# Rotary difference and sum of the softmax heads formed on VectorE instead of GpSimd

## The chip, the cores and the metric

The kernel runs on one core of one Trainium2 chip. A core has five engines that work side by side, each through its own queue of instructions in a fixed order: TensorE (PE in the profile; its weight loads are PEld), VectorE (DVE), ScalarE (ACT), GpSimd (POOL) and SyncE (SP, which here only issues DMAs). The engines wait for each other through semaphores. The metric is the device time of one execution in microseconds (us), lower is better.

## The reference

A trunk of two layers over 512 positions of width 1024, in float32. Each layer has two groups of attention heads side by side on one input projection: eight stick-breaking heads (called s here) and four differential heads (called d), each of which has two softmax maps. Only the d heads get rotary position embedding. An MLP with squared ReLU follows.

```python
def rope(x, pos):
    ...
    x1, x2 = xf[..., : d // 2], xf[..., d // 2:]
    rot = jnp.concatenate([-x2, x1], axis=-1)
    return (xf * cos + rot * sin).astype(x.dtype)

for l in range(DEPTH):
    h = rmsnorm(x, attn_norm[l])
    proj = jnp.einsum('bsd,de->bse', h, w_in[l])
    sb_q, sb_k, sb_v, df_q, df_k, df_v = jnp.split(proj, splits, axis=-1)
    sb_out = stick_breaking_attention(sb_q, sb_k, sb_v)
    dq, dk = rope(df_q, pos), rope(df_k, pos)
    df_heads = differential_attention(dq, dk, dvv, lam)
    ...
    x = x + jnp.einsum('bse,ed->bsd', mixed, w_o[l])
    h = rmsnorm(x, mlp_norm[l])
    u = jnp.square(jax.nn.relu(jnp.einsum('bsd,df->bsf', h, w_ff1[l])))
    x = x + jnp.einsum('bsf,fd->bsd', u, w_ff2[l])
return rmsnorm(x, final_norm)
```

For a pair of halves (x1, x2) rotation gives x1 cos - x2 sin and x2 cos + x1 sin.

## The kernel before

Activations lie transposed, features on the 128 partitions and the 512 positions along the row, so that every projection block is a 128x512 tile. To keep float32 accuracy each operand of a matmul is split in two: a high part of reduced precision, made by ScalarE as a copy (`hi`), and the rest (`lo`), made by VectorE as a subtraction. A product is then three matmuls (`three`, lines 281 to 283). Weights are streamed from memory through SP's queue into buffers named `raw`, split into `whi` (line 116, ScalarE) and `wlo` (line 117, VectorE), and used some 5 us later.

In each layer a list (`ORDER`) interleaves the projection blocks: four d heads (d0 to d3), each followed by its values (w0 to w3), then the s heads. The generator `dense` emits these blocks; between its steps the attention work `attn` of heads that are ready is emitted in small pieces (scores, softmax, transposes, product with the values). A clock of estimated PE time decides where: `defer(delay, fn)` puts work off until that clock has advanced by `delay`, and `ready` says from when a head's scores may be emitted. What is written so is a program text. The order in which each engine runs its instructions is then set by the framework's planner when the program is built: it takes, of the instructions whose inputs and buffers are there by its own estimate, the one that was emitted first.

The step around the change is `evict_d`. For a d head, the projection was arranged so that one block (named q in the tile names) holds the first halves of both maps' queries and keys, and a second block (named k) holds their second halves. For each block VectorE multiplies the result, still in PSUM, with the cosine (`u`, line 445) and with the sine (`v`, line 446). The tables `cos_t` and `sin_t` also hold the normalisation of the input. When the second block has been multiplied, `rest` is deferred by `DLY_R` (3.5 us). It forms `u1 - v` (line 453) and `v1 + u` (line 454), in place in the first block's tiles; splits both into `hl` (line 224 for the high part on ScalarE, line 225 for the rest on VectorE); and moves the pieces by twelve DMAs on SP's queue (line 420) into the tiles `st` (query; and key, high part) and `kl` (key, rest). In the kernel before, lines 453 and 454 run on GpSimd.

The tiles u and v come from a ring of five buffers (tag "t", `TB = 5`) that the products, the values' `tv` tiles and other row tiles share. A new product waits until a buffer is freed, that is, until `rest` of an earlier head has read it.

What stands near it: the scores (lines 477 and 478) of a head on PE wait for `st` and `kl`; the softmax has a masking memset, a maximum (lines 521 to 526), an exponential on ScalarE (534), a reciprocal and small steps (540, 541) and a weighted sum of the two maps (544), which is transposed on PE (567). The norm of a finished d head sends a power of -1/2 through GpSimd (`rc`, line 259), whose result is cast by VectorE (`chi`, line 260, and `clo`, line 261) and spread by GpSimd into two diagonal tiles (264, 266). In the head d3 this norm, of an earlier head, meets the change's step.

Of the kernel before, what the change touches and what calls it, by code (L numbers as in the profile page):

```python
# [151 lines left out]
def trunk(ctx, tc, xT, w, w2, gains, gfin, lamv, cos, sin, out):  # L152
    nc = tc.nc
# [69 lines left out]
    def split(hi, lo, src):  # L223
        nc.scalar.activation(hi, src, AF.Copy)  # L224
        nc.vector.tensor_tensor(out=lo, in0=src, in1=hi.bitcast(F32), op=ALU.subtract)  # L225
# [91 lines left out]
    for l in range(L):  # L317
        with ExitStack() as actx:
# [18 lines left out]
            def tt(name):  # L337
                return a2.tile([P, S], F32, tag="t", name=name, bufs=TB)
# [4 lines left out]
            def parts(name):  # L343
                return a2.tile([P, 2, 2, S], F32R, tag="hl", name=name)
# [62 lines left out]
            def defer(delay, fn):  # L407
                later.append((clock[0] + delay, fn))
                later.sort(key=lambda e: e[0])

            def stack_tiles(kind, b, which):
                nm = f"{l}{kind}{b}{which}"
                out = [a2.tile([P, 2, S], F32R, tag="st" + which, name="st" + nm)]
                if which == "k":
                    out.append(a2.tile([P, 2, S], F32R, tag="kl", name="kl" + nm))
                stacks[(kind, b, which)] = out
                return out

            def move(dst, src):
                nc.sync.dma_start(dst.bitcast(F32), src.bitcast(F32))  # L420
# [21 lines left out]
            def evict_d(pt, kind, b, which):  # L442
                nm = f"{l}{kind}{b}{which}"
                u, v = tt("u" + nm), tt("v" + nm)
                nc.vector.tensor_mul(u, pt, cos_t)
                nc.vector.tensor_mul(v, pt, sin_t)
                if which == "q":
                    heads[("x", b)] = (u, v)
                    return
                u1, v1 = heads.pop(("x", b))  # L450

                def rest():
                    nc.gpsimd.tensor_sub(u1, u1, v)
                    nc.gpsimd.tensor_add(v1, v1, u)
                    q, = stack_tiles(kind, b, "q")
                    k = stack_tiles(kind, b, "k")
                    hl = parts("hl" + nm)
                    for j, o in enumerate((u1, v1)):
                        split(hl[:, 0, j, :], hl[:, 1, j, :], o)
                        to = slice(64 * j, 64 * j + 64)  # L460
                        for m in range(2):
                            rq = slice(32 * m, 32 * m + 32)
                            rk = slice(64 + 32 * m, 64 + 32 * m + 32)
                            move(q[to, m, :], hl[rq, :, j, :])
                            for half in range(2):
                                move(k[half][to, m, :], hl[rk, half, j, :].unsqueeze(1).to_broadcast([32, 2, S]))
                    ready[(kind, b)] = clock[0] + DLY_D

                defer(DLY_R, rest)
# [299 lines left out]
        with ExitStack() as fctx:  # L769
# [152 lines left out]
            for g in range(GROUPS):  # L922
# [26 lines left out]
                for f, form in enumerate(FORMS):  # L949
# [6 lines left out]
                    for n, (c, i, r) in enumerate(work):  # L956
                        if c not in held:
                            held[c] = W.next("f")
                        u = held[c]
# [154 lines left out]
```

## Time and profile before

| | |
|---|---|
| median of 3 runs | 1173.97 us (1173.69 to 1174.61) |
| the profiled execution | 1170.51 us, of which 1168.7 us are the span of the trace |
| granted clock of PE | 0.997 of full speed |
| lines 453 and 454 | 16 instructions, 128x512 each, on GpSimd, from 33.6 to 86.2 us (layer 0) and from 611.6 to 664.3 us (layer 1) |
| DMA | 170.11 MB moved, 146 GB/s on average |

The profile lists one execution. "Busy" is time in which an engine ran an instruction; matmuls overlap each other, so that PE may be recorded as busy a little beyond what it does. A row of the timeline gives the start, the duration, the engine, the line and operation, the tile written and those read, the shape, and in brackets how long the engine had been idle before and what ended the wait. A row of waits gives who waited, for whom, the sum in us, how often and the longest. SPq is the queue that SP issues DMAs from. The tile names carry layer, kind, head and block: `u0d3q` is u of layer 0, head d3, first block; the rows with `1` are layer 1.

### The profile page before, as it was taken

Reading aid. Unit: us, or ns where it says so; the run is one execution under the profiler, and the core shown is the slowest. Engines: PE = TensorE matmul, PEld = TensorE weight load, DVE = VectorE, ACT = ScalarE, POOL = GpSimd, SP = SyncE. Lnnn points to the kernel's source line nnn. Section 1 sums busy time; section 2 is a strip of 40 time slices with the busy share of each in tenths; the row PEclk is TensorE's granted clock in tenths of the full one; section 3 lists DMA queues with packets and bytes.
Section 4 is the critical chain, followed back from the end, with each engine's and each line's share of the span. In section 5 each row is a group of like instructions: output and inputs, shape, how many; then the busy total and the mean of one; then the engine's idle time right before and its main releaser. Section 6 shows DMA issues by size and latency. Waiting matters only on the chain.

```text
span 1168.7 us, 15328 instructions
## 1 busy us (share of the span) xinstructions
PE 1147.7 (98%) x5454; PEld 952.0 (81%) x5454; DVE 813.0 (70%) x1302; ACT 652.4 (56%) x1153; POOL 213.7 (18%) x282
## 2 busy tenths in 40 slices
PE   9999999999999999999899999999999999999996
PEld 6887888888888888888688878888888888888884
DVE  7888788765545756647789877877655466476568
ACT  6455666556756446455445556655666563554554
POOL 1222443130100101002012215331201010010021
PEclk9999999999999999999999999999999999999999
DMA  7555433255844936837525553432658368276185
GB/s 246 163 151 171 123 113 109 72 190 152 212 136 105 224 128 126 224 95 157 110 72 166 168 153 109 140 96 73 225 122 229 120 124 226 93 168 192 36 173 132
DMA packets 56860, 170.11 MB, mean 146 GB/s; under 512 B 7120, under 2 KB 8144, under 8 KB 56784
## 3 DMA queue, kind: packets, MB, share of 16 engines
q1 hardware_dynamic: 46416, 131.88, 34.6%
q0 software_dynamic: 10224, 37.23, 18.5%
q8 instruction: 43, 0.70, 0.2%
q14 instruction: 33, 0.27, 0.1%
q10 hardware_dynamic: 144, 0.02, 0.0%
HBM read 138.17 MB, written 2.10 MB: 120 GB/s over the span
## 4 chain that ended last, share of the span: by engine, by line
PE 86%; DVE 5%; DMA 2%; issue 2%; ACT 1%; POOL 0%; SPq 0%; POOLq 0%; DVEq 0%; ACTq 0%
PE f L282 10%; PE f L283 10%; PE f L281 10%; PE x L282 4%; PE x L281 4%; PE x L283 4%; PE wo L281 3%; PE wo L282 3%; PE wo L283 3%; DMA q<-in_w 2%; DVE wlo L117 1%; PE T0s L567 1%; PE T1s L567 1%; PE O0s L596 0%; PE O1s L596 0%
## 5 line engine op out<-in xcount | busy, mean ns | idle before, releaser
L117 DVE TENSOR_TENSOR wlo<-raw,whi 128x1024 fp32r<-128x1024 f32 (+1 forms) x130 | 154.6, 1193 | 98.0 <-ACT whi L116 97.4
L117 DVE TENSOR_TENSOR wlo<-q,whi 128x512 fp32r<-128x512 f32 x224 | 146.0, 687 | 106.2 <-ACT whi L116 105.7
L281 PE MATMUL f<-h_hi,whi 128*128 128x512 f32 x512 | 199.6, 390 | 0.0
L283 PE MATMUL f<-h_hi,wlo 128*128 128x512 f32 x512 | 199.3, 389 | 0.0
L282 PE MATMUL f<-h_lo,whi 128*128 128x512 f32 x512 | 199.2, 389 | 0.0
L116 ACT ACTIVATE whi<-q 128x512 fp32r<-128x512 f32 x224 | 129.6, 624 | 120.3 <-PE f L282 38.1
L116 ACT ACTIVATE whi<-raw 128x1024 fp32r<-128x1024 f32 (+1 forms) x130 | 131.5, 1018 | 106.7 <-PE f L282 55.4
L794 POOL DMA_DIRECT2D q<-in_w x64 | 56.0, 878 | 558.1 <-DVE wlo L117 471.9
L281 PEld LDWEIGHTS f<-h_hi,whi 128*128 128x128 f32 x512 | 96.1, 188 | 19.9
L282 PEld LDWEIGHTS f<-h_lo,whi 128*128 128x128 f32 x512 | 96.1, 188 | 19.9
L283 PEld LDWEIGHTS f<-h_hi,wlo 128*128 128x128 f32 x512 | 96.1, 188 | 19.9
L225 DVE TENSOR_TENSOR Al<-F,Ah 128x256 fp32r<-128x256 f32 (+2 forms) x96 | 74.8, 779 | 44.1 <-ACT Ah L224 44.0
L281 PE MATMUL x<-whi,Ah 128*128 128x512 f32 x256 | 100.0, 391 | 0.0
L282 PE MATMUL x<-wlo,Ah 128*128 128x512 f32 x256 | 99.8, 390 | 0.1
L283 PE MATMUL x<-whi,Al 128*128 128x512 f32 x256 | 99.7, 389 | 0.0
L224 ACT ACTIVATE Ah<-F 128x256 fp32r<-128x256 f32 (+2 forms) x96 | 67.6, 704 | 45.7 <-DVE F L830 43.7
L282 PEld LDWEIGHTS x<-wlo,Ah 128*128 128x128 f32 x256 | 48.1, 188 | 10.4 <-DVE wlo L117 0.5
L281 PEld LDWEIGHTS x<-whi,Ah 128*128 128x128 f32 x256 | 48.1, 188 | 10.0
L283 PEld LDWEIGHTS x<-whi,Al 128*128 128x128 f32 x256 | 48.1, 188 | 9.9
L821 ACT ACTIVATE F<-f 128x512 f32<-128x512 f32 x64 | 37.6, 587 | 10.9 <-DVE Al L225 5.4
L822 ACT ACTIVATE F<-F 128x512 f32<-128x512 f32 x64 | 40.3, 630 | 1.5
L228 ACT ACTIVATE h_hi<-x,g_all 128x512 fp32r<-128x512 f32 x32 | 22.6, 718 | 26.1 <-DVE x L704 13.8
(1057 smaller groups left out, 2574.1 us busy)
## 6 DMA issues: line engine op xcount, KB each, us to landing
raw<-in_w SPq DMA_DIRECT2D x126, 512.0 KB, 3.5
q<-in_w SPq DMA_DIRECT2D x64, 512.0 KB, 5.5
q<-in_w POOLq DMA_DIRECT2D x64, 512.0 KB, 6.0
x<-in_xT SPq DMA_DIRECT2D x8, 256.0 KB, 4.3
raw<-in_w SPq DMA_DIRECT2D x8, 128.0 KB, 4.2
yx<-y POOLq DMA_DIRECT2D x2, 512.0 KB, 7.8
y<-y POOLq DMA_DIRECT2D x2, 512.0 KB, 7.7
y<-yx POOLq DMA_DIRECT2D x2, 512.0 KB, 6.0
```

What stands on the lines that cost most here:

```text
L116: h = nc.scalar.activation(hi[:, a:b], raw[:, a:b], AF.Copy)
L117: self.last = h, nc.vector.tensor_tensor(out=lo[:, a:b], in0=raw[:, a:b], in1=hi[:, a:b].bitcast(F32), op=ALU.subtract)
L224: nc.scalar.activation(hi, src, AF.Copy)
L225: nc.vector.tensor_tensor(out=lo, in0=src, in1=hi.bitcast(F32), op=ALU.subtract)
L228: a = nc.scalar.activation(h_hi[:, c, :], x[:, c, :], AF.Copy, scale=g)
L281: nc.tensor.matmul(pt, ah, bh, start=first, stop=False)
L282: nc.tensor.matmul(pt, ah, bl, start=False, stop=False)
L283: nc.tensor.matmul(pt, al, bh, start=False, stop=last)
L567: nc.tensor.transpose(pt[:, off : off + P], u["w"][qi][:, kb * P : (kb + 1) * P], ident)
L794: nc.gpsimd.dma_start(t, quad(g, q, c), accum_op=ALU.add)
L821: nc.scalar.activation(t, pt, AF.Relu)
L822: nc.scalar.activation(t, t, AF.Square)
```

## The change

The two operations of `rest` are issued on VectorE. Nothing else in the text is altered; what comes before and after them is emitted at the same places.

```diff
@@ -450,8 +450,8 @@
                 u1, v1 = heads.pop(("x", b))
 
                 def rest():
-                    nc.gpsimd.tensor_sub(u1, u1, v)
-                    nc.gpsimd.tensor_add(v1, v1, u)
+                    nc.vector.tensor_sub(u1, u1, v)
+                    nc.vector.tensor_add(v1, v1, u)
                     q, = stack_tiles(kind, b, "q")
                     k = stack_tiles(kind, b, "k")
                     hl = parts("hl" + nm)
```

## The prediction

> **What bounds the kernel now.** I read the page's head first, then busy time in stretches of 10 us around the two places where the changed lines run, then what TensorE waited for there, and then the queues of each engine in order of time.
>
> ```profile
> span 1168.7 us, 15328 instructions
> PE 1147.7 (98%) x5454; PEld 952.0 (81%) x5454; DVE 813.0 (70%) x1302; ACT 652.4 (56%) x1153; POOL 213.7 (18%) x282
> ...
> 40.00:50.00 10.00, 9.39 (x48) 7.60 (x47) 9.09 (x17) 4.60 (x13) 3.26 (x2) 1.00 0.73 190
> 50.00:60.00 10.00, 9.62 (x50) 7.81 (x48) 9.26 (x25) 6.06 (x16) 1.29 (x1) 1.00 0.76 236
> 60.00:70.00 10.00, 10.00 (x50) 8.49 (x51) 9.97 (x25) 5.76 (x16) 2.20 (x1) 1.00 0.52 139
> ...
> 90.00:100.00 10.00, 8.65 (x46) 6.83 (x45) 8.55 (x18) 5.07 (x9) 0.00 (x0) 1.00 0.77 222
> ```
>
> TensorE (PE) is busy 98% of the span. The rows of stretches give, after the length, PE, weight load, VectorE (DVE), ScalarE (ACT) and GpSimd (POOL). Where the softmax heads are prepared, DVE is nearly full (9.97 of 10 from 60 to 70) while POOL has room. So nothing that POOL or DVE does counts by itself; it counts where PE stands still. That is rare, and it is listed:
>
> ```profile
> PE S0d L477 <- issue: 1.4, 1, 1.4
> PE p0d2q L283 <- DVE wlo L117: 0.6, 1, 0.6
> PE T0d L567 <- DVE p0d L544: 0.4, 1, 0.4
> ...
> PE S1d L477 <- DMA kl1d3k<-hl1d3k: 1.4, 1, 1.4
> PE vT1w L386 <- DVE tv1w L381: 0.2, 1, 0.2
> PE S1d L478 <- DMA kl1d0k<-hl1d0k: 0.2, 1, 0.2
> ```
>
> The first three are from 30 to 100 us (layer 0), the others from 600 to 680 us (layer 1). Together 4.2 us, and that is almost all that this change can win. The two of 1.4 us are the scores of the last softmax head, d3. A recorded wait understates what is lost, because matmuls overlap:
>
> ```profile
> 94.65 0.40 PE L282 MATMUL p0s0q<-h_lo,whi 128*128 128x512 f32 x1
> 94.89 0.40 PE L283 MATMUL p0s0q<-h_hi,wlo 128*128 128x512 f32 x1
> 96.63 0.36 PE L477 MATMUL S0d<-st0d3k,st0d3q 128*128 128x256 f32 x1 [1.35 <-issue]
> ```
>
> Starts are 0.24 apart in the stream, and this one comes 1.74 after the last: 1.5 us are lost, 0.15 more than the wait says. With 0.15 for each of six waits the whole is about 5.1 us, which is the bound of the gain.
>
> **The change part by part.** Sixteen instructions (a difference, line 453, and a sum, line 454, for four heads in two layers) leave POOL and go to DVE. No DMA is added, and no other work.
>
> *Their own cost.* What they take now and what their like takes on DVE:
>
> ```profile
> 40.99 2.27 POOL L453 TENSOR_TENSOR u0d1q<-u0d1q,v0d1k 128x512 f32<-128x512 f32 x1
> 57.84 1.29 POOL L454 TENSOR_TENSOR v0d2q<-v0d2q,u0d2k 128x512 f32<-128x512 f32 x1 [14.58 <-DVE sm0d L540]
> 82.65 1.30 POOL L454 TENSOR_TENSOR v0d3q<-v0d3q,u0d3k 128x512 f32<-128x512 f32 x1 [18.11 <-ACT whi L116]
> 83.90 1.03 POOL L259 TENSOR_TENSOR rc<-ms,mhalf 128x4 f32<-128x4 f32 x1
> 84.90 1.30 POOL L453 TENSOR_TENSOR u0d3q<-u0d3q,v0d3k 128x512 f32<-128x512 f32 x1
> ...
> 38.93 0.68 DVE L445 TENSOR_TENSOR u0d1k<-p0d1k,cos_t 128x512 f32<-128x512 f32 x1
> 39.52 0.68 DVE L446 TENSOR_TENSOR v0d1k<-p0d1k,sin_t 128x512 f32<-128x512 f32 x1
> 40.12 1.99 DVE L117 TENSOR_TENSOR wlo<-raw,whi 128x1024 fp32r<-128x1024 f32 x1
> 42.04 1.77 DVE L225 TENSOR_TENSOR hl0d1k<-v0d1q,hl0d1k 128x512 fp32r<-128x512 f32 x1
> 43.96 0.69 DVE L225 TENSOR_TENSOR hl0d1k<-u0d1q,hl0d1k 128x512 fp32r<-128x512 f32 x1
> 45.17 1.21 DVE L117 TENSOR_TENSOR wlo<-raw,whi 128x1024 fp32r<-128x1024 f32 x1
> 57.99 1.17 DVE L541 SCALAR_TENSOR_TENSOR sm0d<-top,nlam,sm0d 128x1 f32<-128x1 f32 x1
> 60.65 0.22 DVE L541 SCALAR_TENSOR_TENSOR sm0d<-top,nlam,sm0d 128x1 f32<-128x1 f32 x1
> ```
>
> A 128x512 operation on DVE records 0.68 and starts 0.60 after the one before it, so two cost DVE 1.2 us for each head, 4.8 us a layer. Against that stands what the POOL ones cost DVE today. While line 453 runs (40.99 to 43.26), the weight split wlo takes 1.99 instead of 1.21 and the split of hl 1.77 instead of 0.69: 1.9 us lost at d1. At d2 a one-element step takes 1.17 instead of 0.22 beside line 454, 0.95 lost; I estimate the same once more beside line 453 of d2, so 1.9. At d3 it is the cast chi, below, about 1 us. At d0 DVE only waits for buffers that POOL frees, 0.8 us. Sum 5.6 us a layer against 4.8 us: DVE does not get fuller. That is my first choice, and it decides the sign.
>
> The Trainium skill, page "SBUF — State Buffer", section "Who interferes with whom", says that a VectorE instruction with two SBUF inputs and a GpSimd instruction that reads SBUF shut each other out for the whole instruction, whichever starts first. The long rows of wlo and hl agree (1.99 and 1.77). But by the same rule the moved operations, which have two SBUF inputs, can be held by the POOL work that stays, such as rc: at d3 that would make the gain 1.0 a layer, and the sum below 2.2 instead of 2.6.
>
> *Head d3, both layers.* The chain that ends in the 1.5 us stall:
>
> ```profile
> 82.58 0.67 DVE L446 TENSOR_TENSOR v0d3k<-p0d3k,sin_t 128x512 f32<-128x512 f32 x1
> 84.97 1.25 DVE L260 CAST chi<-rc 128x4 fp32r<-128x4 f32 x1 [1.72 <-POOL rc L259]
> 86.13 0.54 DVE L522 TENSOR_REDUCE sm0d<-S0d 128x1 f32<-128x384 f32 x1
> ...
> 91.17 0.69 DVE L225 TENSOR_TENSOR hl0d3k<-v0d3q,hl0d3k 128x512 fp32r<-128x512 f32 x1
> ...
> 93.89 0.54 SPq L420 DMA_DIRECT2D st0d3q<-hl0d3k  x1
> ...
> DMA to landing us min/median/max: 2.7/2.7/2.8
> ```
>
> The query tile's last needed piece is issued at 93.89 and takes 2.7 us: 96.6, where the scores start. The issues follow each other at about 0.6 us from the moment the rest hl is split, so the start is set by DVE's queue. There DVE stood idle for 1.72 us, because POOL ran line 454 (82.65 to 83.95) before rc, and then chi took 1.25 beside line 453 (a like cast without POOL beside it is priced by its size, 128x4, near the 0.22 of the small step above). Afterwards: rc starts at about 82.65 and ends at 83.7; DVE runs the two moved operations from 83.2 to 84.4 in that gap; chi needs 0.2 and the reduction L522 begins at about 84.6 instead of 86.13, which is 1.5 earlier; if the first moved operation has to stand behind rc, to 83.7, it is 1.0 earlier. With the order kept, the hl split, the DMAs and the scores move by 1.0 to 1.5, against a stall of 1.5. I take 1.2, as the hold is likelier in part than in full. Two layers: 2.4 (2.0 to 3.0). Late next are the key's low parts, which follow at the same pace.
>
> *Head d1.* The stall on wlo in layer 0 goes if wlo keeps its place and runs 1.21 from 40.12. But behind it the scores of d0 wait for their own moves:
>
> ```profile
> 34.97 0.69 DVE L445 TENSOR_TENSOR u0d1q<-p0d1q,cos_t 128x512 f32<-128x512 f32 x1 [0.28 <-POOL v0d0q L454]
> ...
> 35.63 2.43 SPq L420 DMA_DIRECT2D st0d0k<-hl0d0k  x3
> ...
> 40.75 0.55 SPq L420 DMA_DIRECT2D st0d0q<-hl0d0k  x1
> ...
> 43.88 0.28 PE L477 MATMUL S0d<-st0d0k,st0d0q 128*128 128x256 f32 x1
> ```
>
> At d0 POOL starts at once when an operand is there (u0d1q above is released at 34.97), while on DVE the first one stands behind the values' product and ends about 0.35 later, at 35.3. The moves run without a gap from 35.63 on, so all of them come 0.35 later: the query lands at 40.75 + 2.7 + 0.35 = 43.8. Of the stall of 0.6 (0.78 with overlap) only 0.1 is won in layer 0 (0 to 0.78); in layer 1, where the scores of d0 already wait 0.2, 0.35 is lost (0 to 0.35).
>
> *Head d2.* The wait of 0.4 (0.5 lost) for p0d stands directly behind the step that took 1.17 instead of 0.22. I take 0.5 won (0 to 0.5). The queries' products there and the softmax steps then share DVE with two more operations; their cover is the time given back by POOL, and if that fails they cost up to 1.2.
>
> *Sum:* 2.4 + 0.1 - 0.35 + 0.5 = 2.65, say 2.6 us. Against the profiled execution's own 1170.51 us (span 1168.7 and 1.8 around it) that gives 1167.9. The median of the runs is 1173.97, 3.5 above the profiled one, so I set the sum against it: **1171.4 us**. Bounds of this case: 2.0 - 0.35 = 1.6 and 5.1.
>
> **The rivals.** *All stalls go* (1169.5): the planner puts the hl splits of d3 well ahead, and the small waits go too, 4.5 of the 5.1. For it: the high half of u0d3q would be ready near 85 instead of 88. Against it: d0, which gets later.
>
> *The stall moves and little is left* (1173.0): the hl splits stay behind the softmax steps of d2, or layer 0's gain is lost again at the end of its dense part, where PE's next work hangs on a transfer:
>
> ```profile
> 548.79 8.27 DMA q<-in_w
> ```
>
> This piece of the chain of waits is a DMA of 8.27 us. It follows work of DVE that itself follows PE, so I expect it to move along; if it doesn't, only layer 1's half remains, about 1.0.
>
> *DVE becomes the bound* (1178.8, slower). The order on each engine is set when the program is built: line 454 ran before line 453 although the text has them the other way round. If the planner puts the two operations in front of the weight rest (wlo) at d1, and in front of the softmax steps at d2, then PE waits for them with no slack, as it does today at p0d2q and at T0d. 1.2 us in four blocks (d1 and d2, two layers) is 4.8 us, with d3 no better. It decides from the point where what POOL gave back (1.9 us in each of these blocks) is less than 1.2 at the place that PE waits for. For it: DVE at 9.97 of 10. Against it: the balance of 5.6 against 4.8.
>
> **How the numbers follow.** Forecast 0.45, all stalls gone 0.15, little left 0.13, DVE the bound 0.27. The forecast's own range is 1168.9 to 1172.4. Less than 0.2% (2.35 us) cannot be told from no change in a measurement of this kernel; of the forecast's 0.45 about 0.33 lies beyond that. Faster 0.33 + 0.15 = 0.48; no difference 0.12 + 0.13 = 0.25; slower 0.27. The range for 8 in 10 reaches from 1168.5, a little past the bound of 5.1, to 1177.0, most of the way to the slower case, leaving about 0.15 above and little below.
>
> **What would show it.** Lines 453 and 454 on DVE at about 0.68 each; wlo near 40 us at 1.2 and not 2; the one-element step at d2 at 0.2; chi at about 0.2 and its wait for rc under 1 us; the last query move of d3 issued by 92.9 or sooner; the wait of S0d and S1d for d3 under 0.5. Against it would speak a wait of PE for wlo or p0d of over 1 us, moves of d0 that begin more than 0.5 later, or an order on DVE that differs far beyond the moved lines. The forecast is wrong if the d3 stalls stay, or if new waits of PE add up to what they gave.

## The result and the profile after

The changed kernel takes 1167.25 us in the median of 7 runs (1164.61 to 1168.64), the kernel before 1173.97 us in 7 (1170.33 to 1176.40): a ratio of 0.9943, interval 0.9925 to 0.9961, so 4.6 to 8.8 us less. The prediction was 1171.4 us; it had the sign right, but the time lies below its range (1168.5 to 1177.0). A second measurement on another occasion gave 0.9957 (0.9941 to 0.9973). The changed kernel's profiled execution took 1167.25 us, of which 1165.4 are the span.

The busy time by stretch, first of the kernel before and then of the kernel after (columns as in the prediction: length, PE, weight load, DVE, ACT, POOL):

```profile
30.00:110.00 80.00, 77.60 (x398) 64.44 (x398) 70.14 (x148) 40.90 (x96) 17.38 (x12) 1.00 0.56 158
...
600.00:690.00 90.00, 88.21 (x446) 73.12 (x445) 75.67 (x163) 43.86 (x101) 19.51 (x15) 1.00 0.55 154
```

```profile
30.00:110.00 80.00, 80.00 (x413) 67.21 (x412) 70.38 (x162) 41.05 (x98) 5.92 (x6) 1.00 0.57 166
...
600.00:690.00 90.00, 88.63 (x451) 73.61 (x450) 75.21 (x174) 43.06 (x103) 8.27 (x8) 1.00 0.54 158
```

PE has no idle time left in layer 0 (77.60 to 80.00 of 80) and little less than before in layer 1. DVE is as full as it was (70.14 and 70.38; 75.67 and 75.21), although it runs 16 instructions more; POOL has lost 11 us in each layer. That balance was foretold. Now the waits of PE in the kernel after (those from start-up and from the dense layers' ends left out):

```profile
PE rs_m L940 <- POOL ssq L238: 1.3, 2, 0.7
...
PE vT1w L386 <- DVE tv1w L381: 0.7, 1, 0.7
PE S1d L477 <- issue: 0.6, 1, 0.6
```

All three waits of layer 0 (1.4, 0.6 and 0.4) are gone; in layer 1 two of 0.7 and 0.6 stand in the place of 1.4, 0.2 and 0.2. The first line is for the sum of squares behind the output projection. It is not the change's doing: a second profile of the kernel after has no such wait, and a second one of the kernel before has one of 0.7 (see the last section). Of the other two the second profile shows only S1d, with 0.5.

Where head d3 is prepared, the timeline of the kernel after shows this:

```profile
82.33 0.17 DVE L260 CAST chi<-rc 128x4 fp32r<-128x4 f32 x1 [0.93 <-POOL rc L259]
...
84.64 0.66 DVE L446 TENSOR_TENSOR v0d3k<-p0d3k,sin_t 128x512 f32<-128x512 f32 x1
...
87.74 0.66 DVE L453 TENSOR_TENSOR u0d3q<-u0d3q,v0d3k 128x512 f32<-128x512 f32 x1
...
88.93 0.67 DVE L454 TENSOR_TENSOR v0d3q<-v0d3q,u0d3k 128x512 f32<-128x512 f32 x1
...
92.97 0.54 SPq L420 DMA_DIRECT2D st0d3q<-hl0d3k  x1
93.56 0.60 SPq L420 DMA_DIRECT2D st0d3k<-hl0d3k  x1
...
96.44 0.47 PE L477 MATMUL S0d<-st0d3k,st0d3q 128*128 128x256 f32 x2
```

The two operations take 0.66 and 0.67, as foretold, and chi 0.17 instead of 1.25. But they don't run at once: their last operand is there at 85.30 and the difference starts at 87.74, 2.4 us later, behind softmax steps and a weight rest that were emitted earlier. The query's third move is issued at 92.97, close to the 92.9 that the prediction asked for, and yet the scores start at 96.44, where they started at 96.63 before. The moves have changed their order too. In the kernel before, all four of the key's high part went ahead of the query's:

```profile
84.64 4.53 SPq L420 DMA_DIRECT2D st0d3k<-hl0d3k  x4
```

Now the third of them, which the first scores need as well, is issued behind the query's third, at 93.56. With the 2.7 us that these moves take to land, the last piece is there at about 96.3, where it was there at 96.6 before: 0.3 us earlier, not 1.2. The gain is what PE did until then. This is the last matmul of each K step of block p0s0q (duration minimum, median, maximum in ns; first and last start), of the kernel before and of the kernel after:

```profile
L283 PE MATMUL p0s0q<-h_hi,wlo x8: 389/389/397, 90.3 to 97.5; 128*128 128x512 f32 x8
```

```profile
L283 PE MATMUL p0s0q<-h_hi,wlo x8: 389/390/397, 88.9 to 94.2; 128*128 128x512 f32 x8
```

Before, PE stood in front of the scores with three matmuls of p0s0q still to do. Afterwards the last matmul of that block starts at 94.2, and PE has begun the next block when it comes to the scores. The scores have been given a later place in PE's queue:

```
before                                          after
430 L477 S0d<-st0d3k,st0d3q                      430 L281 p0s0q<-h_hi,whi
431 L281 p0s0q<-h_hi,whi                         431 L282 p0s0q<-h_lo,whi
432 L282 p0s0q<-h_lo,whi                         432 L283 p0s0q<-h_hi,wlo
...                                              ...
438 L477 S0d<-st0d3k,st0d3q                      443 L477 S0d<-st0d3k,st0d3q
439 L281 p0s0k<-h_hi,whi                         444 L477 S0d<-st0d3k,st0d3q
```

That is 13 places. The program text emits PE's work in the same order in both kernels; the planner, which counts the two operations among DVE's work, has reordered PE's queue around the d heads of both layers.

### The profile page after: what moved, and what is told of

It reads as the page before. It is cut to its first block, busy times and chain, and to the rows that moved or that the text cites. A ratio compares the mean times of both kernels' runs of the same rounds, so it can differ in the third digit from the quotient of the medians.

```text
span 1165.4 us, 15309 instructions
## 1 busy us (share of the span) xinstructions
PE 1146.1 (98%) x5454; PEld 951.3 (82%) x5454; DVE 818.5 (70%) x1318; ACT 650.4 (56%) x1153; POOL 184.4 (16%) x266
## 4 chain that ended last, share of the span: by engine, by line
PE 87%; DVE 5%; DMA 3%; issue 2%; ACT 2%; POOL 1%; SPq 0%; POOLq 0%; ACTq 0%; DVEq 0%
PE f L283 10%; PE f L281 10%; PE f L282 10%; PE x L282 4%; PE x L281 4%; PE x L283 4%; DMA q<-in_w 2%; PE wo L281 2%; PE wo L282 2%; PE wo L283 2%; DVE wlo L117 1%; DVE h_lo L229 1%; ACT whi L116 1%; PE T0s L567 1%; PE T1s L567 1%
```

## The experiments

All ratios are to the kernel before, with their 95% intervals. Two theories were set against each other: D, the prediction's, that the data of a head come earlier; and P, that the planner's new order of TensorE is the gain.

**The two kernels again** (unchanged).

> The kernel before, unchanged, profiled a second time and timed in five rounds: ratio 1.000 within 0.2%. It tells what one profile of it is worth. Theory S (sample): its profiled execution of 1170.5 was a quick one, and most executions carry about 3 us of waits of TensorE that the first profile does not show; then an execution near 1174 shows TensorE waits of 3 us more than the 4.2 us around the softmax heads and the 12 us elsewhere. Theory H (heads): the waits around the heads are those of the first profile, and the rest of the gap between 1170.5 and 1174 is spread thin over the whole span.

> The changed kernel, profiled a second time and timed in five rounds. The first measurement was a ratio of 0.9943. If that is a property of the kernel, 0.992 to 0.997 again, 4 to 9 us below the kernel before; if it was the spread of single executions, about 0.9975, the 3.3 us by which the two profiles differ.

The kernel before: 0.9994 (0.9983 to 1.0005), profiled execution 1171.50. The kernel after: 0.9957 (0.9941 to 0.9973), 1168.16. The gain is the kernel's own. Theory S was not put to its test, because the second profiled execution of the kernel before, 1171.50, was not one near 1174 either; it shows the same waits around the heads, with one of 0.7 for the sum of squares besides. Both pairs of profiles differ by 3.3 us. The medians differ by 6.7 on the first occasion; on the second by 4.6 (1172.31 against 1167.67), or by 5.5 against all 23 executions of the kernel before there.

A part of this spread goes with the granted clock. Over all 58 executions of the kernel before that were taken beside the experiments, the 21 at a clock of 0.997 took 1172.3 in the mean and the 9 at 0.994 took 1174.3. Both profiles of the kernel before were taken at 0.997, the second one of the kernel after at 0.994: at equal clock its 1168.16 stand against 1174.3. For the first pair (0.997 and 0.999) this is no explanation; there it stays open.

**One layer alone** (both lines written with a condition on the layer).

```diff
-                    nc.gpsimd.tensor_sub(u1, u1, v)
-                    nc.gpsimd.tensor_add(v1, v1, u)
+                    (nc.vector if l == 0 else nc.gpsimd).tensor_sub(u1, u1, v)
+                    (nc.vector if l == 0 else nc.gpsimd).tensor_add(v1, v1, u)
```

> Difference and sum on VectorE in layer 0 alone. The order of the instructions of layer 1 is then that of the kernel before. Theory of the prediction (data come earlier, half the gain in each layer): half of the whole, about 3 us. Rival (the waits of TensorE in layer 0, all gone in the changed profile, are the gain; layer 1 only exchanges its waits): 2.5 to 4 us or more in layer 0, that is 60 to 90% of the whole.

> Difference and sum on VectorE in layer 1 alone; layer 0 has the order of the kernel before. Theory of the prediction: the other half, about 3 us. Rival: 0 to 1.5 us, since two new waits of 0.7 and 0.6 us replace one of 1.4. The two halves should add up to the change as a whole; if they don't, the layers act on each other through the transfers between them.

Layer 0 alone: 0.9952 (0.9938 to 0.9967), 5.6 us. Layer 1 alone: 0.9973 (0.9960 to 0.9985), 3.2 us. Each layer that keeps POOL keeps its waits. In the first of these kernels:

```profile
PE S1d L477 <- issue: 1.6, 1, 1.6
```

and in the second:

```profile
PE S0d L477 <- issue: 1.4, 1, 1.4
...
PE p0d2q L283 <- DVE wlo L117: 0.6, 1, 0.6
PE T0d L567 <- DVE p0d L544: 0.4, 1, 0.4
...
PE S1d L477 <- issue: 0.5, 1, 0.5
```

Neither theory holds in both layers. Layer 0 gives more than the 3 us that the prediction's theory had for it, as the rival said; layer 1 gives about the 3 us of that theory and not the rival's at most 1.5. The halves make more than the whole, 0.48% and 0.27% against 0.43% and 0.57% in its two measurements; each of these figures has an interval of 0.12 to 0.18% on either side, so that this is at the edge of the noise and stays open.

**Engine and order taken apart.** TensorE's order was held, instruction for instruction, by order-only dependencies between neighbours in its queue, over the stretches in which the two kernels differ. The other engines' orders are left to the planner.

```diff
+    for runs in PE_ORDER:
+        names = [f"I-{n}" for a, b in runs for n in range(a, b + 1)]
+        for a, b in zip(names, names[1:]):
+            behind(nc.made[b], nc.made[a])
```

> Difference and sum stay on GpSimd; TensorE's order is held to that of the changed kernel, instruction for instruction, in both places where the two orders differ. Theory P (the planner's order of TensorE is the gain: the scores of a head stand later in its queue, behind dense matmuls that need nothing from the head): most of the gain, 4 to 5.5 us, 0.9950 to 0.9965. Theory D (the data of the heads come earlier, as the prediction had it): little of it, 0 to 1.5 us, since the data come when they came before; a later place of the scores alone saves only what was waited.

> Difference and sum on VectorE; TensorE's order is held to that of the kernel before. Theory P: the waits for the scores of d3 and for the weight rest come back, gain 0 to 1.5 us (0.9985 to 1.0). Theory D: the waits of 1.4 us at d3 are under 0.5, gain 3 us or more, 0.9975 or less, and it is the prediction's sum measured by itself (2.6 us).

| | order of before | order of after |
|---|---|---|
| difference and sum on GpSimd | 1 (the kernel before) | 0.9963 (0.9951 to 0.9975) |
| on VectorE | 1.0048 (1.0029 to 1.0066) | 0.9957 and 0.9943 (the change) |

The order alone, with no instruction moved to another engine, gives 4.3 us. The move alone, with TensorE's order kept, costs 5.6 us. Theory P stands and D falls, further than expected: with the old order the data come later on DVE.

Three limits go with this table. No kernel was held to its own order, so that what the holding does to the other engines' queues is not measured by itself. The executions with VectorE and the old order had a mean granted clock of 0.993, those of the kernel before beside them 0.995; against all 58 of the kernel before at equal clock they are 3.4 us slower (0.994: 1177.7 in 2 executions against 1174.3 in 9) and 2.6 us slower (0.996: 1175.6 in 1 against 1173.0 in 12). The loss is clear, its size less so. And the two effects don't simply add: the new order is worth 4.3 us with GpSimd and 11 to 12 with VectorE, and the engine, which costs under the old order, costs nothing under the new one. It may even give something there: the last matmul of block p0s3q, behind the d heads of layer 0, starts at 174.8 and 175.2 in the two profiles of the kernel before, at 171.8 and 172.0 in those of the kernel after, and at 173.6 with the new order alone. In layer 0 the order alone thus made about half of what the change made there.

Waits of PE in the kernel with the move and the old order:

```profile
PE S0d L156 <- DMA kl0d3k<-hl0d3k: 1.9, 1, 1.9
...
PE S1d L156 <- DMA st1d3q<-hl1d3k: 1.8, 1, 1.8
...
PE S1d L156 <- DMA st1d2k<-hl1d2k: 1.2, 1, 1.2
...
PE S0d L156 <- DMA st0d0q<-hl0d0k: 0.8, 1, 0.8
PE S0d L156 <- DMA st0d2k<-hl0d2k: 0.8, 1, 0.8
```

These five are for scores of a head, at d0, d2 and d3. Those at d3 have grown from 1.4 to 1.9 and 1.8. Its timeline says why:

```profile
84.14 0.67 DVE L473 TENSOR_TENSOR v0d3k<-p0d3k,sin_t 128x512 f32<-128x512 f32 x1
...
89.84 0.68 DVE L480 TENSOR_TENSOR u0d3q<-u0d3q,v0d3k 128x512 f32<-128x512 f32 x1
```

The difference starts 5.0 us after its operand is there (84.81). At d3 DVE's order is here, but for one split, that of the kernel before, with the two operations put in shortly ahead of the splits that need them, behind the softmax steps, and not in the gap. POOL, idle for 18 us, had started the sum, the first of the pair, within 0.2 us of its operand, and the difference 1.7 us after its own. And the mirror image, POOL with the new order, has small waits only, among them the old one for wlo, which POOL's contention with DVE makes:

```profile
PE p0d2q L156 <- DVE wlo L117: 0.6, 1, 0.6
PE T1d L161 <- DVE p1d L571: 0.3, 1, 0.3
...
PE S0d L156 <- ACT p0d L561: 0.2, 1, 0.2
```

**Head d3 alone** (the same condition, with `b == 3`).

> Only head d3 of each layer on VectorE. Theory D: the two waits of 1.4 us go and the others stay: 2 to 3 us. Theory P: what counts is whether TensorE's order around d3 changes; it changes there in some 40 places, so 1.5 to 3 us too; the profile tells them apart by when the scores of d3 start (earlier than 96.6 us: D; about 96.6 with more dense matmuls done by then: P).

0.9968 (0.9957 to 0.9980), 3.8 us: by the median more than either theory had, though the interval reaches down to 2.3. Of the early waits these two stay:

```profile
PE p0d2q L283 <- DVE wlo L117: 0.6, 1, 0.6
PE T0d L567 <- DVE p0d L544: 0.4, 1, 0.4
```

The scores of d3 start at 97.17, not earlier than before but 0.5 later, and the last matmul of block p0s0q starts at 95.7 instead of 97.5. By the mark set, that is P: the gain at d3 is a matter of order too.

**The operations emitted at once.** They stand right behind the second block's products in the text, no longer in `rest`.

```diff
+                nc.vector.tensor_sub(u1, u1, v)
+                nc.vector.tensor_add(v1, v1, u)
+
                 def rest():
-                    nc.vector.tensor_sub(u1, u1, v)
-                    nc.vector.tensor_add(v1, v1, u)
```

> Difference and sum on VectorE, emitted right behind the second block's products instead of 3.5 us later with the rest, so that they stand ahead of softmax steps and weight rests in VectorE's queue; the planner orders TensorE as it likes. If the place of the scores in TensorE's queue is the whole gain (theory P), this is the changed kernel again within 1.5 us, unless the weight rests come late: 0.993 to 0.997. Rival (the prediction's slower case: the two operations go ahead of the weight rest, and TensorE waits for that): 2 to 5 us more than the changed kernel, with waits of TensorE for wlo.

> The same, with TensorE's order held to that of the kernel before. With that order the deferred operations cost 5.6 us, where the prediction had counted a gain of 2.6. If the step that failed is that they don't run at once, but 2 to 4 us behind their operands because they are emitted late and VectorE takes earlier work first, then emitting them at once brings the gain that was predicted: 0 to 3 us, 0.9975 to 1.0. If VectorE is simply too full for them, it stays slower: 1.002 to 1.006.

With the planner's own order 0.9972 (0.9958 to 0.9985): a gain, probably smaller than the change's. The profile shows a wait of 0.9 for wlo at p0d2q, where wlo starts at 41.03 instead of 40.07, so the two operations do delay the weight rest, but by less than the rival had it. With the old order 0.9993 (0.9983 to 1.0004): the 5.6 us are gone, and no difference can be told. That the late start made the loss is thus confirmed; the gain of 2.6 us that was predicted lies outside the interval, so starting early doesn't bring it. The timeline of this kernel at d3:

```profile
82.29 0.67 DVE L471 TENSOR_TENSOR v0d3k<-p0d3k,sin_t 128x512 f32<-128x512 f32 x1
...
84.69 0.68 DVE L477 TENSOR_TENSOR u0d3q<-u0d3q,v0d3k 128x512 f32<-128x512 f32 x1
85.29 1.52 DVE L478 TENSOR_TENSOR v0d3q<-v0d3q,u0d3k 128x512 f32<-128x512 f32 x1
...
84.91 1.35 POOL L291 TENSOR_TENSOR dgld<-edge,clo 128x512 fp32r<-128x512 f32 x1 [0.16 <-PE S0d L156]
...
96.01 0.36 PE L156 MATMUL S0d<-st0d3k,st0d3q 128*128 128x256 f32 x1 [1.04 <-issue]
```

The difference now runs 1.7 us behind its operand instead of 5.0, and the scores start at 96.0 instead of 96.6. But the sum takes 1.52 instead of 0.68, because POOL spreads the norm's diagonals at that time, and the transposes of the values come late: PE waits 0.8 for `tv` in each layer.

**A later emission of the scores**, nothing else (`DLY_D` 10 for 8).

> The kernel before, with difference and sum on GpSimd, but the scores of the d heads are emitted when the planner's clock is 10 us past the rest instead of 8 (DLY_D). Theory P: a later place of the scores in TensorE's queue is worth something without moving anything to VectorE: 1 to 4 us, 0.9965 to 0.999. Rival: the order that the planner makes after a move is as good or bad by chance, 0.998 to 1.003.

1.0004 (0.9991 to 1.0018): no gain, as the rival had it. The two waits at d3 are gone, and two others have come in their place:

```profile
PE S1d L477 <- DMA st1d2q<-hl1d2k: 1.9, 1, 1.9
...
PE rb_d L274 <- issue: 1.4, 2, 0.7
```

A later place by itself is not the gain; what is shown is that the one order that the planner made with the change is. Which of its places matter is not shown.

**The sum of squares on VectorE as well** (`add_sq(db, db == 0, tt, nc.vector)` in the output projection, on top of the change).

> The changed kernel, and also the running sum of squares after the output projection (14 additions of 128x512) on VectorE instead of GpSimd. In the changed kernel these additions meet two-operand subtractions of VectorE, which then take 1.8 us instead of 0.75, and TensorE waits up to 0.7 us in each layer for the last one. Theory: 0 to 1.4 us less than the changed kernel. Rival: VectorE has to carry 8.4 us more where the output projection already needs it, and h is late: 1 to 3 us more than the changed kernel.

0.9948 (0.9936 to 0.9960), median 1166.56: its profile has no wait for the sum of squares, but neither has the second profile of the changed kernel, and the time can't be told from the changed kernel's 0.9943 and 0.9957.

## Why the prediction was off

- **Own cost on DVE: right.** 0.66 to 0.68 each, and not held by the POOL work that stays; emitted at once under the old order, one of them was (1.52). The load was balanced as worked out: DVE busy for 70.4 us of the 80 at layer 0's heads, against 70.1.
- **The contention given back: right, but for a reading.** wlo at 40 us took 1.21 instead of 1.99, chi 0.17 instead of 1.25, and no one-element step at d2 took over 0.21. The waits at p0d2q and T0d went; the first stays with the new order alone, so it was POOL's, while the second goes with the order alone. The long wlo was put down to line 453. It starts at 40.12, when line 454 still runs, to 41.03, so that its 0.8 us belong to line 454; line 453 held the split behind it. What POOL kept still holds DVE: at d3 of the kernel after a weighted sum of 128x256 (line 544, at 82.88) takes 1.09 beside one of the norm's diagonals, and 0.47 at 52.51, where POOL is idle.
- **Head d3, "with the order kept, the hl split, the DMAs and the scores move by 1.0 to 1.5": wrong, in both its halves.** This is the step that failed, and it carried 2.4 of the 2.6 us. The order was not kept: the sum has no term for a new order of PE's queue, which alone gives 4.3 us. And the data don't come 1.2 earlier. In the changed kernel it is 0.3 at layer 0, because the third move of the key's high part has become the last that the first scores need; with PE's order kept, the scores wait longer than before (1.9 and 1.8 instead of 1.4). "DVE runs the two moved operations from 83.2 to 84.4 in that gap" took their start to be set by their operands. On POOL, which was idle, that was so for the first of the two. On DVE their turn came 2.4 us later in the changed kernel and 5.0 under the old order. Instead of 2.6 won, the move alone costs 5.6 us. In so far as the right sign rested on this step, it is luck.
- **Head d0, "about 0.35 later": right in kind, too small.** The first move is issued at 36.73 instead of 35.63, 1.1 later. The query's third is issued as before, at 40.72, but the third of the key's high part only at 41.31, so that the first scores' last piece comes 0.6 later; under the old order PE waits 0.8 there. In the changed kernel those scores, too, were moved back in PE's queue, so that nothing was lost. So the sum for d1, 0.1 of the stall's 0.78, was too small: the last matmul of block p0d2q starts 0.9 and 0.8 earlier in the two pairs of profiles.
- **The rivals.** The measured time is closest to "all stalls go" (4.5 us), but its reason, that the hl splits of d3 come well ahead, is not what happened. "DVE becomes the bound" had 4.8 us as its price; the kernel with the order kept lost 5.6, though in waits for the scores and not for wlo and p0d. So the slower case has the size of the engine's effect under the old order, and the planner's new order, 11 to 12 us the other way by the ratios, made the result.
- **The bound of 5.1 us** was the sum of six waits in one execution. The medians differ by 6.7, and by 4.6 to 5.5 on the second occasion, with intervals that reach below 5.1; the range should not have ended just past the bound. The prediction did name "an order on DVE that differs far beyond the moved lines" as a sign against it. It was one.

## What to carry to other kernels

Where a planner orders the queues, a move from one engine to another is two changes, and the second, the new order, can be larger than the first and of the other sign, and the two need not add up: predict it as a case of its own, and test it by holding the order. Work moved from an idle engine to a busy one doesn't start when its operands are there but when its turn comes; look at what was emitted ahead of it. A wait of the bounding engine can be removed by bringing the data earlier or by asking for them later: here the second did most of it at d3, though asking later at another place won nothing.

## What the runs showed of the hardware

That POOL and DVE hold each other up was foretold from the rows; new is that it has a lasting rhythm, and that the rhythm belongs to the execution and not to the kernel. In the first profile of the kernel after, behind the output projection, the timeline shows:

```profile
248.23 1.54 DVE L117 TENSOR_TENSOR wlo<-raw,whi 128x1024 fp32r<-128x1024 f32 x1
249.69 1.76 DVE L229 SCALAR_TENSOR_TENSOR h_lo<-x,g_all,h_hi 128x512 fp32r<-128x512 f32 x1
...
249.53 1.37 POOL L238 TENSOR_TENSOR ssq<-ssq,sq 128x512 f32<-128x512 f32 x1 [0.85 <-ACT sq L237]
```

In its second profile the same instructions of the same kernel meet the other way round:

```profile
247.80 0.75 DVE L229 SCALAR_TENSOR_TENSOR h_lo<-x,g_all,h_hi 128x512 fp32r<-128x512 f32 x1
...
247.90 1.79 POOL L238 TENSOR_TENSOR ssq<-ssq,sq 128x512 f32<-128x512 f32 x1 [1.47 <-ACT sq L237]
```

In these rows the one that starts first, by 0.1 to 0.2 us, keeps about its time (0.75 and 1.37), and the other takes 1.0 or 0.5 longer. The kernel before shows both rhythms too: 0.75 on DVE with 1.80 on POOL in its first profile, 1.77 on DVE in layer 0 of its second and 0.75 in layer 1. In the rhythm in which DVE is held, PE paid 0.7 us, in both layers of the first profile of the kernel after and in one layer of the second profile of the kernel before; in the other rhythm it paid nothing. What sets the rhythm is not shown.
